# Sequence 1's ends behind the loop, and ScalarE and VectorE in written order, in the second MLP products of an encoder trunk

## The chip, the cores and the metric

The kernel runs on one core of a Trainium2 chip. The metric is the device time of one execution in microseconds (us). TensorE is PE, VectorE is DVE, ScalarE is ACT, GpSimd is POOL and SyncE is SP.

## The reference, cut to what matters

Two sequences (q = 0 and 1) of 512 tokens and 1024 features pass through two layers. Layer 0 mixes by a Fourier transform, layer 1 by attention. Each is followed by an MLP with squared ReLU:

```python
def sq_relu_mlp(h, w_up, w_down):
    a = jnp.maximum(h @ w_up, 0)
    return (a * a) @ w_down

for i in range(DEPTH):
    x = x + (fourier_mix(...) if i == 0 else gqa_attention(rms_norm(x, ...), ...))
    x = x + sq_relu_mlp(rms_norm(x, mlp_norm[i]), w_up[i], w_down[i])
return rms_norm(x, final_norm)
```

The change lies in the product with `w_down` of both layers and in what follows it: the QKV projection of layer 1's attention behind layer 0, a last small projection and the final norm behind layer 1.

## The kernel before

Every matmul of the MLP is done three times on a 128x512 tile. A 32-bit operand is split into a rounded high half and the rest, the low half: ACT copies the high half, then DVE subtracts it (`split`, lines 85 to 87). The product is high x high, high x low and low x high (`product`, line 907), with the weights stationary, so the third matmul of a product is the first to read the weights' low half.

The two sequences are not multiplied apart. Weights and activations are seen as 2 x 2 blocks, and seven products of sums of blocks take the place of eight. For the second MLP product these are `b11` and `b21` (class `Row`: two products of 12 matmuls) and `t1`, `t3`, `t2`, `b22`, `t4` (class `Sums`: five products, 60 matmuls). `second_product` goes over four groups of the inner dimension and, in each, over four column blocks m = 0 to 3. One turn of its loop is an item: the sums of one m, and in most items a row product of an m of the next group. In the last group the item of m = 1 has the last row (84 matmuls), those of m = 2 and 3 have none (60 each).

Within an item the weights of the next one are made ready. Three transfers fetch its raw blocks into a pool of five tiles. Then `sum_23` (two subtractions on DVE, lines 1183 and 1184), `split_12`, `sum_4` (line 1190), `split_4` and `split_3` follow. `split_3` makes `s3`, which the second product of the next item reads, and `a22`, which the fifth reads. Results leave PSUM by DVE adds (line 1113). One of the five goes to `e[m]`, a part that three blocks of the residual share. `xs[q, m]` is the residual; when all is done for a column block, `finish(m)` adds `e[m]` to one half of `xs[0, m]` (line 1253) and to both halves of `xs[1, m]` (line 1254), and calls `ready(m)`.

In layer 0 `ready` makes, for both sequences, the two halves of the operand `hT` of the QKV projection (`make_h`: a scaled copy on ACT, line 90, and DVE's half, line 91) and the squares for its norm (ACT, line 160, added up on POOL, line 164), and parks the residual in HBM on SP's queue (line 193). In the same last steps `late` fetches the four tiles of the weights of v (line 1359) and splits them.

Behind the loop `begun` does six of the eight steps of the inner dimension for v and k of sequence 0 (72 matmuls), then `token_scale` sums the squares (line 172), and a loop over the tiles finishes the projection, sequence 0 first.

Most of the order is found by a list scheduler, which simulates the engines and takes, engine by engine, the earliest instruction in program order that is ready. Inside `tc.manual_schedule(engines=...)` the instructions of the engines named keep the order in which they are written; others may still be placed between them. In the loop of `second_product` only PE is held so.

Of the kernel before, what the change touches and what calls it, by code (L numbers as in the profile page):

```python
# [12 lines left out]
F32 = mybir.dt.float32  # L13
# [6 lines left out]
P = 128  # L20
D = 1024
S = 512
NSEQ = 2
NT = S // P
KC = D // P
# [19 lines left out]
def trunk_kernel(ctx, tc, x_in, xt_in, y_out, tables, rope, gfour, gcol, grow, gfin,  # L45
                 w_four, w_nyq, w_qkv, w_o, w_a22, w_up, w_row2, w_row4, w_sum2, w_sum4, w_down):
    nc = tc.nc
# [17 lines left out]
    def slot(shape, dt):  # L65
        return act.tile(shape, dt, tag="u4", name=nm("u"))
# [18 lines left out]
    def split(dst_hi, dst_lo, src, eng=nc.vector):  # L85
        nc.scalar.copy(dst_hi, src)  # L86
        eng.tensor_sub(dst_lo, src, f32(dst_hi))  # L87
# [23 lines left out]
    def lent():  # L111
        return slot([P, 1024], F32R), slot([P, 1024], F32R)
# [32 lines left out]
    xs, acc, apart = {}, {}, {}  # L145
# [38 lines left out]
    def make_h(q, fo, g0):  # L184

        h = slot([P, 2, 512], F32R)
        split_scaled(h[:, 0], h[:, 1], xt(q, fo), gc[:, g0 + fo : g0 + fo + 1])
        return h
# [3 lines left out]
    def put_away(q, i):  # L192
        nc.sync.dma_start(park[q, i], xs[q, i])
# [507 lines left out]
    ET = mybir.EngineType  # L701
    with tc.manual_schedule(engines={ET.PE, ET.Activation, ET.DVE, ET.Pool, ET.SP}):
# [128 lines left out]
        blocks = Blocks(0)  # L831
# [259 lines left out]
                pass  # L1091
            pairs[-1].out(*done, nc.vector)

    def second_product(l, blocks, rows, late=lambda: None, ready=lambda m: None):
        e, new = [], [True] * 4
        there = set()

# [152 lines left out]
        def finish(m):  # L1250
            left[m] -= 1
            if left[m] == 0:
                nc.vector.tensor_add(xs[0, m][:, 1], xs[0, m][:, 1], e[m])
                nc.vector.tensor_add(xs[1, m], xs[1, m], e[m].unsqueeze(1).broadcast_to([P, 2, 512]))
                ready(m)

        first_product(l, blocks, rows, ahead)
# [36 lines left out]
        def hook():  # L1294
            for x in later:
                x[0] += 1
            if later and later[0][0] > 2:
# [2 lines left out]
                put(op, h)  # L1300
                held[op] = g

        for k, (rows, sums) in enumerate(items):
            nrows, nsums = items[k + 1] if k + 1 < len(items) else ([], None)
            end = sums.m if sums.g == len(GROUPS[l]) - 1 else -1
            if end in (0, 2):
                late()
            with tc.manual_schedule(engines={ET.PE}):
                for r in rows:
                    r.first()  # L1310
                    if r.m == 3:
                        change("b11", r.g)
                for r in nrows:
                    r.load()
                hook()
                for i, op in enumerate(("t1", "t3", "t2", "b22", "t4")):
                    sums.go(i)
                    if sums.m == 3:
                        change(op, sums.g)
                    if i == 0 and nsums:  # L1320
                        nsums.load()
                    if i == 1:
                        for r in rows:
                            r.second()
                            if r.m == 3:
                                change("b21", r.g)
                        if end == 1:
                            late()
                            late()
                        hook()  # L1330
                        for r in nrows:
                            r.split()
                    if i == 4 and nsums:
                        nsums.split_3()
                    hook()
                    if k == 0 and i in (2, 4):
                        change(ROW[i // 4], 0)
                    if i == 2 and nsums:
                        nsums.sum_23()
                        nsums.split_12()  # L1340
                    if i == 3 and nsums:
                        nsums.sum_4()
                        nsums.split_4()
            for r in rows:
                finish(r.m)
            finish(sums.m)


    hT, rs, wkv = [[], []], [], []
# [5 lines left out]
        rs.append(r)  # L1355

    def late():
        raw = slot([P, 1024], F32)
        nc.sync.dma_start(raw, w_qkv[2, len(wkv)])
        wkv.append(lent())  # L1360
        split(*wkv[-1], raw)

    def ready(m):
        for q in range(NSEQ):
            for fo in range(2 * m, 2 * m + 2):
                hT[q].append(make_h(q, fo, KC))
                square(q, fo)
            put_away(q, m)

    second_product(0, blocks, rows, late, ready)  # L1370

    gb = tm((P, 4, HD))
    nc.sync.dma_start(gb, grow.to_broadcast([P, 4, HD]))
# [197 lines left out]
    transposes = {(0, 0, 0): 0, (0, 1, 0): 1}  # L1571

    begun = [qkv(2, 0, t, wkv, 0, KC - 2) for t in range(NT)]
    token_scale(0)
    keeping, turned = keep(), iter(())
    ws = {2: wkv}
# [18 lines left out]
    def tile_qkv(cg, q, t):  # L1595
        if (cg, q, t) in transposes:
            transpose_k(transposes[cg, q, t])
        if (cg, q) == (2, 0):
            o = qkv(cg, q, t, ws[cg], KC - 2, KC, begun[t])
        else:  # L1600
            o = qkv(cg, q, t, ws[cg])
        if (cg, q, t) == (2, 0, 0):
            token_scale(1)
        r = rs[q][:, t : t + 1]
        if cg == 2:
            split_scaled(vt[q][0][:, t], vt[q][1][:, t], o[:, 256:], r)
            return norm_rope(o, NKV, rt["k"], [t], [kr[q][:, t]], scale=r)
        outs = [qr[q, 2 * cg + i][:, t] for i in range(2)]
        if (cg, q, t) != (1, 1, 1):
            return norm_rope(o, 4, rt["q"], [t], outs, scale=r)  # L1610
        raw = slot([P, 512], F32)
        nc.scalar.activation(raw, o, AF.Copy, scale=r)
        return norm_rope(raw, 4, rt["q"], [t], outs)
# [84 lines left out]
    with tc.manual_schedule(engines={ET.PE}):  # L1698
# [56 lines left out]
                blocks.first_lo(j - 3)  # L1755
        for i in range(2, 4):
            blocks.first_lo(i)
    second_product(1, blocks, rows)
    ats = []
    for f in range(2 * PLAIN):  # L1760
        raw = load_raw(plain[f], (P, 2, 512))
# [60 lines left out]
    with tc.manual_schedule(engines={ET.PE, ET.Activation, ET.DVE, ET.Pool, ET.SP}):  # L1822
        oa, ob, oc, oe = OutT(0, 4), OutT(1, 2), Out(2), Out(3)
        for fo in range(KC):
            project(0, fo, ws, [a[0] for a in ats])
            square(0, fo)
            oa.gain(fo)
        xtok = [tokens(2), tokens(3)]
        for fo in range(KC):
            project(1, fo, ws, [a[1] for a in ats], 256)  # L1830
            square(1, fo, 256, fo == KC - 1)
            ob.gain(fo)
            if fo == 1:
                oa.root()
            if fo == 3:
                oa.spread()
            if fo > 3:
                oa.write(fo - 4)

        x, z = xtok  # L1840
        y = slot([P, D], F32), slot([P, D], F32)
        groups = ((0, 512), (512, 768), (768, 1024))

        def tile(t, c0, c1, at=0, mid=lambda: None):
            o = ps()[:, : c1 - c0]
            for k in range(len(ats)):
                ak, wk = ats[k][1], ws[k]
                cols = slice(t * P, (t + 1) * P)
                mm3(o, ak[0][:, cols], ak[1][:, cols], wk[0][:, c0:c1], wk[1][:, c0:c1], k == 0, k == len(ats) - 1)
                if k == at:  # L1850
                    mid()
            return o

        def add(x, o, c0, c1):
            nc.vector.tensor_add(x[:, c0:c1], o, x[:, c0:c1])

        def write(x, y, r, i):
            sl = slice(i * 512, i * 512 + 512)
            nc.vector.scalar_tensor_tensor(y[:, sl], x[:, sl], r, gf[:, sl], ALU.mult, ALU.mult)

        o = [tile(2, 0, 512, 2, ob.root)]
        add(x, o[0], 0, 512)
        o.append(tile(2, 512, 1024, 0, ob.spread))
        oc.square(x[:, :512], 0)
        ob.write(0)
        add(x, o[1], 512, 1024)
        oc.square(x[:, 512:], 1)
        o = [tile(3, 0, 512)]
        ob.write(1)
        ob.write(2)  # L1870
        root = oc.root(1)
        for step in root[:2]:
            step()
        ob.write(3)
        for step in root[2:]:
            step()
        add(z, o[0], *groups[0])
        oe.square(z[:, :512], 0)
        write(x, y[0], oc.r, 0)
        o += [tile(3, *g) for g in groups[1:]]  # L1880
        add(z, o[1], *groups[1])
        oe.square(z[:, 512:768], 1)
        write(x, y[0], oc.r, 1)
        nc.sync.dma_start(y_out[2][:P], y[0])
        root = oe.root(2)
        add(z, o[2], *groups[2])
        oe.square(z[:, 768:], 2)
        nc.vector.tensor_mul(y[1][:, 512:768], z[:, 512:768], gf[:, 512:768])
        root[0]()
        root[1]()  # L1890
        nc.vector.tensor_mul(y[1][:, 768:], z[:, 768:], gf[:, 768:])
        for step in root[2:]:
            step()
        nc.scalar.activation(y[1][:, 512:], y[1][:, 512:], AF.Copy, scale=oe.r)
        nc.scalar.dma_start(y_out[2][P:, 512:], y[1][:, 512:])
        write(z, y[1], oe.r, 0)
        nc.sync.dma_start(y_out[2][P:, :512], y[1][:, :512])
# [151 lines left out]
```

## Time and profile before

| | |
|---|---|
| three runs | 1680.71, 1683.82, 1684.49 us; median 1683.82 |
| profiled execution | 1682.5 us, span 1680.5 us |
| granted TensorE clock, mean | 0.998 |
| PE busy | 1666.0 us, 99% of the span |
| DVE, ACT, POOL busy | 1258.9, 873.4, 394.5 us |

A timeline row gives start, duration, engine, line of the kernel, operation, output<-inputs, shapes and count; in brackets stands the idle time of the engine before it and what ended it. A row of the windows gives, for a stretch, its length, the busy time of PE, PE's weight load (PEld), DVE, ACT and POOL (with instructions), the granted clock of TensorE, the share of the DMA engines and GB/s. A row of the waits gives total, number of times and longest.

### The profile page before, as it was taken

Reading aid. Unit: us, or ns where it says so; the run is one execution under the profiler, and the core shown is the slowest. Engines: PE = TensorE matmul, PEld = TensorE weight load, DVE = VectorE, ACT = ScalarE, POOL = GpSimd, SP = SyncE. Lnnn points to the kernel's source line nnn. Section 1 sums busy time; section 2 is a strip of 40 time slices with the busy share of each in tenths; the row PEclk is TensorE's granted clock in tenths of the full one; section 3 lists DMA queues with packets and bytes.
Section 4 is the critical chain, followed back from the end, with each engine's and each line's share of the span. In section 5 each row is a group of like instructions: output and inputs, shape, how many; then the busy total and the mean of one; then the engine's idle time right before and its main releaser. Section 6 shows DMA issues by size and latency. Waiting matters only on the chain.

```text
span 1680.5 us, 22279 instructions
## 1 busy us (share of the span) xinstructions
PE 1666.0 (99%) x7845; PEld 1387.7 (83%) x7845; DVE 1258.9 (75%) x1848; ACT 873.4 (52%) x1537; POOL 394.5 (23%) x364
## 2 busy tenths in 40 slices
PE   9999999999999999999999999999999999999998
PEld 8988888888888888788878888888888888888887
DVE  8879776557786779869888877777855487878865
ACT  6766444456343425447698854554544553433334
POOL 3321443221000001325544303004422220000002
PEclk9999999999999999999999999999999999999999
DMA  9843655459775757425501146334544696757532
GB/s 310 262 151 111 209 194 182 145 176 371 242 231 170 254 171 225 168 65 196 168 1 39 63 164 224 124 114 160 209 156 155 226 367 203 232 158 237 176 102 100
DMA packets 122047, 302.99 MB, mean 180 GB/s; under 512 B 12200, under 2 KB 13352, under 8 KB 121936
## 3 DMA queue, kind: packets, MB, share of 16 engines
q1 hardware_dynamic: 98576, 254.05, 43.6%
q0 software_dynamic: 8960, 21.05, 5.9%
q10 hardware_dynamic: 14400, 26.48, 4.2%
q8 instruction: 61, 1.00, 0.2%
q14 instruction: 50, 0.41, 0.1%
HBM read 218.11 MB, written 82.38 MB: 179 GB/s over the span
## 4 chain that ended last, share of the span: by engine, by line
PE 87%; DVE 6%; ACT 3%; issue 2%; DMA 2%; POOL 0%; SPq 0%; DVEq 0%; ACTq 0%; POOLq 0%
PE ps L907 69%; PE ps L83 5%; PE ps L81 5%; PE ps L82 5%; PE ps L1482 1%; DVE w L87 1%; ACT t L1474 1%; ACT u L86 1%; DVE u L87 1%; DVE u L219 1%; DVE u L235 1%; DVE u L1113 0%; DMA u<-w_four 0%; DMA u<-x 0%; PE ps L172 0%
## 5 line engine op out<-in xcount | busy, mean ns | idle before, releaser
L907 PE MATMUL ps<-u,w 128*128 128x512 f32 x4944 | 1133.3, 390 | 2.9 <-DVE w L87 2.1
L907 PEld LDWEIGHTS ps<-u,w 128*128 128x128 f32 x4944 | 927.5, 188 | 199.1 <-DVE w L87 3.2
L86 ACT CAST w<-raw 128x1024 fp32r<-128x1024 f32 (+1 forms) x216 | 214.0, 996 | 310.9 <-PE ps L907 229.0
L87 DVE TENSOR_TENSOR w<-raw,w 128x1024 fp32r<-128x1024 f32 (+1 forms) x216 | 252.3, 1172 | 77.6 <-ACT w L86 77.3
L86 ACT CAST u<-u 128x1024 fp32r<-128x1024 f32 x144 | 145.2, 1049 | 83.8 <-PE ps L907 36.5
L87 DVE TENSOR_TENSOR u<-u,u 128x1024 fp32r<-128x1024 f32 x144 | 173.3, 1230 | 19.0 <-ACT u L86 17.9
L907 PE MATMUL ps<-u,u 128*128 128x512 f32 x600 | 143.1, 389 | 0.1
L1142 POOL DMA_DIRECT2D raw<-w_sum x32 | 27.7, 866 | 469.3 <-DMA raw<-w_sum 197.9
L1113 DVE TENSOR_TENSOR u<-ps,u 128x512 f32<-128x512 f32 x160 | 109.6, 686 | 37.2 <-PE ps L907 34.4
L1023 POOL TENSOR_TENSOR u<-u 128x512 f32<-128x512 f32 x28 | 37.7, 1345 | 424.7 <-ACT u L920 424.7
L907 PEld LDWEIGHTS ps<-u,u 128*128 128x128 f32 x600 | 112.5, 188 | 23.8 <-ACT u L938 0.5
L81 PE MATMUL ps<-u,u 128*128 128x512 f32 (+2 forms) x340 | 128.8, 381 | 0.4 <-ACT t L1474 0.3
L82 PE MATMUL ps<-u,u 128*128 128x512 f32 (+2 forms) x340 | 124.2, 366 | 0.4 <-DVE u L87 0.3
L83 PE MATMUL ps<-u,u 128*128 128x512 f32 (+2 forms) x340 | 124.4, 366 | 0.1
L164 POOL TENSOR_TENSOR t<-t,t 128x512 f32<-128x512 f32 (+1 forms) x54 | 77.8, 1446 | 190.6 <-ACT t L160 189.9
L919 ACT ACTIVATE t<-t 128x512 f32<-128x512 f32 x64 | 40.5, 632 | 109.8 <-DVE t L992 99.8
L87 DVE TENSOR_TENSOR u<-ps,u 128x512 fp32r<-128x512 f32 (+3 forms) x112 | 68.5, 635 | 7.9 <-ACT u L86 7.3
L83 PEld LDWEIGHTS ps<-u,u 128*128 128x128 f32 x340 | 64.2, 189 | 10.5 <-DVE u L448 0.5
L81 PEld LDWEIGHTS ps<-u,u 128*128 128x128 f32 x340 | 64.3, 189 | 10.1 <-ACT u L86 1.5
L82 PEld LDWEIGHTS ps<-u,u 128*128 128x128 f32 x340 | 64.4, 189 | 9.2 <-DVE u L87 1.4
L979 DVE TENSOR_TENSOR t<-ps,u 128x512 f32<-128x512 f32 x32 | 22.0, 688 | 60.5 <-PE ps L907 52.7
L1476 POOL TENSOR_SCALAR t<-t,s 128x512 f32<-128x512 f32 x64 | 47.3, 740 | 74.0 <-DVE s L1475 60.1
(260 smaller groups left out, 2029.7 us busy)
## 6 DMA issues: line engine op xcount, KB each, us to landing
raw<-w_up SPq DMA_DIRECT2D x80, 512.0 KB, 4.6
u<-spill_t SPq DMA_DIRECT2D x60, 512.0 KB, 6.8
raw<-w_sum SPq DMA_DIRECT2D x56, 512.0 KB, 5.7
u<-spill_b SPq DMA_DIRECT2D x45, 512.0 KB, 6.2
spill_t<-u SPq DMA_DIRECT2D x84, 256.0 KB, 2.0
spill_b<-t ACTq DMA_DIRECT2D x60, 256.0 KB, 4.3
raw<-w_row SPq DMA_DIRECT2D x28, 512.0 KB, 5.2
park<-u SPq DMA_DIRECT2D x24, 512.0 KB, 4.5
```

Of the source, the lines that this page charges most:

```text
L81: nc.tensor.matmul(out, lh, rh, start=first, stop=False)
L82: nc.tensor.matmul(out, lh, rl, start=False, stop=False)
L83: nc.tensor.matmul(out, ll, rh, start=False, stop=last)
L86: nc.scalar.copy(dst_hi, src)
L87: eng.tensor_sub(dst_lo, src, f32(dst_hi))
L164: nc.gpsimd.tensor_add(acc[q][:, :n], acc[q][:, :n], s[:, :n])
L907: nc.tensor.matmul(o, w[x][:, sl], h[k][y], start=first and k + i == 0, stop=k == n - 1 and i == 2, skip_group_check=not first)
L919: nc.scalar.activation(t, src, AF.Relu)
L1023: eng.tensor_sub(t[:, 0], b12, b11)
L1113: nc.vector.tensor_add(x, o, x)
L1142: nc.gpsimd.dma_start(s[:, 1], w[:, 3], accum_op=ALU.add)
L1476: nc.gpsimd.tensor_scalar(p, p, sm_[:, :1], 1.0, ALU.mult, ALU.mult)
```

## The change

- The add of `e[m]` to `xs[1, m]` leaves `finish` and becomes a function `other(m)`, which `second_product` returns. In layer 0 `other` and `ready(m, 1)` are called for all four m behind `begun`; in layer 1 `other` is called in the first four steps of the last projection.
- `ready(m)` now does one sequence, and its square comes ahead of its `make_h`.
- In the items of m = 1, 2 and 3 of the last group ACT and DVE are held in written order like PE. The `finish` of an item's column blocks is written after the first product of the next item, and that of the last item behind the loop.
- `late` becomes a generator. Its five steps stand in the items of m = 1 (one), m = 2 (one) and m = 3 (three); each asks for one tile of v's weights and splits the tile asked for a step before.
- `token_scale(1)` moves behind the first tile of sequence 1.

```diff
-    def second_product(l, blocks, rows, late=lambda: None, ready=lambda m: None):
+    def second_product(l, blocks, rows, late=iter(()), ready=lambda m: None):
...
                 nc.vector.tensor_add(xs[0, m][:, 1], xs[0, m][:, 1], e[m])
-                nc.vector.tensor_add(xs[1, m], xs[1, m], e[m].unsqueeze(1).broadcast_to([P, 2, 512]))
                 ready(m)
...
+        done = []
         for k, (rows, sums) in enumerate(items):
             nrows, nsums = items[k + 1] if k + 1 < len(items) else ([], None)
             end = sums.m if sums.g == len(GROUPS[l]) - 1 else -1
-            if end in (0, 2):
-                late()
-            with tc.manual_schedule(engines={ET.PE}):
+            with tc.manual_schedule(engines={ET.PE, ET.Activation, ET.DVE} if end > 0 else {ET.PE}):
...
                     if i == 0 and nsums:
                         nsums.load()
+                    if i == 0 and end > 0:
+                        for m in done:
+                            finish(m)
+                        done = []
+                    if (end, i) in ((2, 0), (3, 0), (3, 1), (3, 2)):
+                        next(late, None)
                     if i == 1:
...
                         if end == 1:
-                            late()
-                            late()
+                            next(late, None)
                         hook()
...
-            for r in rows:
-                finish(r.m)
-            finish(sums.m)
+            done += [r.m for r in rows] + [sums.m]
+            if end < 0:
+                for m in done:
+                    finish(m)
+                done = []
+        with tc.manual_schedule(engines={ET.Activation, ET.DVE}):
+            for m in done:
+                finish(m)
+
+        def other(m):
+            nc.vector.tensor_add(xs[1, m], xs[1, m], e[m].unsqueeze(1).broadcast_to([P, 2, 512]))
+
+        return other
...
     def late():
-        raw = slot([P, 1024], F32)
-        nc.sync.dma_start(raw, w_qkv[2, len(wkv)])
-        wkv.append(lent())
-        split(*wkv[-1], raw)
-
-    def ready(m):
-        for q in range(NSEQ):
-            for fo in range(2 * m, 2 * m + 2):
-                hT[q].append(make_h(q, fo, KC))
-                square(q, fo)
-            put_away(q, m)
-
-    second_product(0, blocks, rows, late, ready)
+        raw = []
+        for u in range(5):
+            if u < 4:
+                raw.append(slot([P, 1024], F32))
+                nc.sync.dma_start(raw[u], w_qkv[2, u])
+            if u:
+                wkv.append(lent())
+                split(*wkv[-1], raw[u - 1])
+            yield
+
+    def ready(m, q=0):
+        for fo in range(2 * m, 2 * m + 2):
+            square(q, fo)
+            hT[q].append(make_h(q, fo, KC))
+        put_away(q, m)
+
+    other = second_product(0, blocks, rows, late(), ready)
...
     begun = [qkv(2, 0, t, wkv, 0, KC - 2) for t in range(NT)]
+    with tc.manual_schedule(engines={ET.Activation, ET.DVE}):
+        for m in range(4):
+            other(m)
+        for m in range(4):
+            ready(m, 1)
     token_scale(0)
...
-        if (cg, q, t) == (2, 0, 0):
+        if (cg, q, t) == (2, 1, 0):
             token_scale(1)
...
-    second_product(1, blocks, rows)
+    other = second_product(1, blocks, rows)
...
             oa.gain(fo)
+            if fo < 4:
+                other(fo)
```

## The prediction

> **What bounds the kernel now.** I read the page first, then the waits of TensorE (PE), then the windows, then PE and VectorE (DVE) in order of time around the only large wait.
>
> ```profile
> span 1680.5 us, 22279 instructions
> PE 1666.0 (99%) x7845; PEld 1387.7 (83%) x7845; DVE 1258.9 (75%) x1848; ACT 873.4 (52%) x1537; POOL 394.5 (23%) x364
> PE ps L907 <- DVE w L87: 2.1, 2, 1.9
> ```
>
> PE is busy for 99% of the span, so an edit pays only where it shortens a wait of PE, and costs only where it makes one. The largest wait is 1.9 us on a weight split of DVE (line 87). In time it lies here:
>
> ```profile
> 693.71 0.84 PE L907 MATMUL ps<-u,w 128*128 128x512 f32 x3
> 696.46 12.34 PE L907 MATMUL ps<-u,w 128*128 128x512 f32 x46 [1.91 <-DVE w L87]
> 708.64 0.39 PE L81 MATMUL ps<-u,u 128*128 128x512 f32 x1
> 724.96 0.95 PE L172 MATMUL ps<-ones,t 128*128 128x2 f32 x8
> 694.04 1.22 DVE L1254 TENSOR_TENSOR u<-u,t 128x1024 f32<-128x1024 f32 x1
> 695.19 1.22 DVE L87 TENSOR_TENSOR w<-raw,w 128x1024 fp32r<-128x1024 f32 x1
> ```
>
> From 708.64 to 724.96 run the 72 matmuls of `begun`: 0.2267 us each, the pace of an undisturbed PE. The three matmuls from 693.71 end their turn at 694.39; the next starts at 696.46, which is 2.07 late, when the split at 695.19 ends. On DVE an add for sequence 1 (line 1254) went ahead of it. The 46 matmuls from there to 708.64 take 12.18 us, where 46 x 0.2267 is 10.43: another 1.75 is lost. The windows show to what:
>
> ```profile
> 697.00:698.00 1.00, 1.00 (x5) 0.81 (x4) 0.96 (x3) 0.18 (x1) 0.00 (x0) 0.84 1.18 320
> 700.00:701.00 1.00, 1.00 (x4) 0.80 (x3) 0.69 (x1) 0.02 (x1) 1.00 (x1) 0.50 0.79 168
> 702.00:703.00 1.00, 1.00 (x6) 0.81 (x6) 0.00 (x0) 0.00 (x0) 1.00 (x2) 1.00 0.70 287
> ```
>
> The granted clock (the figure ahead of the DMA share) is 0.50 up to 701, and 1.00 again by 702. So this place costs 2.07 + 1.75 = 3.82 us, and no edit here can win much more. 46 matmuls before the loop's end is the third matmul of the second product of the last item (m = 3): the first that needs the low half which `split_3` makes. That item would have begun 14 x 0.2267 earlier, at 691.2, the one before it (60 matmuls) at 677.6, and the one with the last row (84) at 658.6. This is layer 0; layer 1 has no such wait.
>
> **What the change takes away.** In layer 0, from these items, four adds of 1.22 (line 1254) and, for sequence 1, eight split halves on DVE, eight squares and eight scaled copies on ScalarE (ACT) and seven adds on GpSimd (POOL). The add at 694.04 is one of them. The wait of 2.07 and its 1.75 of low clock go if nothing takes their place: -3.82.
>
> **What the written order adds.** In the last three items DVE must now do: the add of the third product, `sum_23`, `split_12`, the add of the fourth, `sum_4`, `split_4`, the add of the fifth, `split_3`, where the scheduler before was free to do the sums for the next item as soon as their weights had come. Durations, from the item before (m = 0) in the same loop, DVE, then ACT:
>
> ```profile
> 652.85 0.69 DVE L1184 TENSOR_TENSOR raw<-raw 128x512 f32<-128x512 f32 x1
> 653.45 0.69 DVE L1113 TENSOR_TENSOR t<-ps,t 128x512 f32<-128x512 f32 x1
> 654.05 0.68 DVE L1190 TENSOR_TENSOR raw<-raw,raw 128x512 f32<-128x512 f32 x1
> 654.70 1.23 DVE L87 TENSOR_TENSOR w<-raw,w 128x1024 fp32r<-128x1024 f32 x1
> 656.71 0.69 DVE L87 TENSOR_TENSOR w<-raw,w 128x512 fp32r<-128x512 f32 x1
> 657.32 1.22 DVE L1254 TENSOR_TENSOR u<-u,t 128x1024 f32<-128x1024 f32 x1
> 653.61 1.06 ACT L86 CAST w<-raw 128x1024 fp32r<-128x1024 f32 x1 [1.94 <-DVE raw L1184]
> 656.06 0.62 ACT L86 CAST w<-raw 128x512 fp32r<-128x512 f32 x1 [1.39 <-PE ps L907]
> 1621.53 0.69 DVE L1113 TENSOR_TENSOR u<-ps,u 128x512 f32<-128x512 f32 x1 [0.41 <-PE ps L907]
> 1624.05 0.39 PE L81 MATMUL ps<-u,w 128*128 128x512 f32 x1
> ```
>
> An add or a 512-wide step lets the next begin after 0.60 (653.45 to 654.05), a 1024-wide split after about 1.14; an instruction that reads the result of the one before waits for its end (0.69); ACT starts 0.07 after the sum it needs (653.54 to 653.61), DVE 0.03 after ACT (654.67 to 654.70). An add starts 0.20 after its product: the product before the last ended 12 x 0.2267 ahead of 1624.05, at 1621.33, and its add began at 1621.53. Counted from the end of the third product: add starts 0.20; `sum_23` starts 0.80, its second half 1.49, ends 2.18; ACT's copy for `split_12` 2.25 to 3.31; DVE's half 3.34, next at 4.48; add of the fourth to 5.08; `sum_4` ends 5.76; ACT's copy 5.83 to 6.45; DVE's half 6.48, next at 7.09; add of the fifth (its product ended at 5.44) to 7.69; `split_3` ends 8.91. What a late low half costs is seen in layer 1's projection, where a split that ends late holds one matmul:
>
> ```profile
> 1625.34 1.22 DVE L87 TENSOR_TENSOR w<-raw,w 128x1024 fp32r<-128x1024 f32 x1
> 1626.62 0.19 PEld L83 LDWEIGHTS ps<-u,w 128*128 128x128 f32 x1 [0.34 <-DVE w L87]
> 1626.95 0.39 PE L81 MATMUL ps<-u,w 128*128 128x512 f32 x1
> ```
>
> It ends at 1626.56; the matmul due at 1624.05 + 11 x 0.2267 = 1626.54 slips and its follower starts at 1626.95, not 1626.77: 0.18 lost. So the loss is the split's end plus 0.16 less the due time. In the new order the third matmul of the next item's second product is due 24 + 14 matmuls after the third product: 8.61. Loss 8.91 + 0.16 - 8.61 = 0.46 us. This chain stands in items m = 1 and m = 2 of both layers, so four times. Two of its steps wait for ACT (1.16 and 0.72).
>
> Two of the four are worse. In layer 0, m = 2, `finish(1)` and the first weight of v stand ahead. From the item's start: add of the first product 2.92, `finish` add to 4.21, ACT square and scaled copy to 5.5, DVE's half to 6.2, split of the weight to 7.6, add of the second to 8.2: just under the 8.36 at which the third's add can start. But a POOL add beside it stretches DVE's work on SBUF operands:
>
> ```profile
> 685.09 7.77 POOL L164 TENSOR_TENSOR t<-t,t 128x512 f32<-128x512 f32 x4 [14.58 <-ACT t L160]
> 687.69 2.31 DVE L87 TENSOR_TENSOR w<-raw,w 128x1024 fp32r<-128x1024 f32 x1
> 689.93 1.78 DVE L91 SCALAR_TENSOR_TENSOR u<-u,gc,u 128x512 fp32r<-128x512 f32 x1
> 684.71 0.75 DVE L91 SCALAR_TENSOR_TENSOR u<-u,gc,u 128x512 fp32r<-128x512 f32 x1
> ```
>
> The half of 0.75 took 1.78 there and the split of 1.22 took 2.31. One POOL add still falls there: between 0 and 0.75; I take 0.3, since it overlaps only one step. In layer 1, m = 2, the scheduler may still place the splits of `ats`, which are not in written order, into the two waits for ACT:
>
> ```profile
> 1597.38 1.06 ACT L86 CAST u<-raw 128x1024 fp32r<-128x1024 f32 x1 [1.95 <-DMA raw<-plain]
> 1601.99 1.21 DVE L87 TENSOR_TENSOR u<-raw,u 128x1024 fp32r<-128x1024 f32 x1
> ```
>
> One that fits the wait of 1.16 costs nothing; one that meets an add costs its 1.14 and delays ACT's copy besides. Ends 0 and 1.3; I take 0.4, nearer the fitting one, as each comes with its own transfer and only one or two meet the chain. Together: 4 x 0.46 + 0.3 + 0.4 = 2.54.
>
> **What is moved and stays hidden.** Sequence 1 now follows the loop, beside the 16.3 us of `begun`, 0.8 of sums and 5.4 of the rest of q = 0: its h is first read 22.6 us after the loop. DVE needs until 3.9 for the last `finish`, 4.6 for the four adds, ACT from 5.2 on about 1.2 for each of eight squares and copies, to 14.8; DVE's last half to 17, or 23 if POOL stretched all eight to 1.78, while the last of them is read only 4 us after the first. Cost 0. DVE has the room:
>
> ```profile
> 720.00:730.00 10.00, 10.00 (x54) 8.55 (x53) 4.07 (x21) 1.22 (x5) 0.00 (x0) 1.00 0.18 52
> 1629.90 0.69 DVE L891 TENSOR_TENSOR u<-ps,u 128x512 f32<-128x512 f32 x1 [2.06 <-PE ps L83]
> ```
>
> In layer 1 the four adds go into the projection, where DVE idles 2.06 between two adds and each takes 1.22: 0. The parking of sequence 1 on SP's queue goes later with its data; behind it stand only loads of the QKV stage. The weights of v are asked for a step ahead:
>
> ```profile
> 696.85 0.64 SPq L1359 DMA_DIRECT2D u<-w_qkv  x1
> 703.59 1.05 ACT L86 CAST u<-u 128x1024 fp32r<-128x1024 f32 x1 [3.57 <-DMA u<-w_qkv]
> ```
>
> Before, the last came 6.7 after its issue, ACT idled 3.57 for it, and PE did not wait. Now ACT and DVE stand still behind such a split, but in the last item only adds follow it, and the banks these free are not needed by `begun`. Cost 0, and 0 gained.
>
> **Sum.** -3.82 + 2.54 = -1.28. The profiled execution took 1682.5 (span 1680.5 and 2.0 around it), so 1681.2 against it. It lies 1.3 below the median of 1683.82; the four executions shown average 1682.9, and against that the forecast is 1681.6.
>
> **A rule beside the rows.** The clock fell after a gap of 1.91 (above) and not after one of 0.73:
>
> ```profile
> 1047.32 0.96 PE L907 MATMUL ps<-u,w 128*128 128x512 f32 x3 [0.73 <-DVE u L1688]
> 1048.00:1049.00 1.00, 1.00 (x6) 0.82 (x5) 1.00 (x2) 0.63 (x2) 0.93 (x1) 1.00 0.00 0
> ```
>
> So none of the four new waits as priced should lower it, and one that grows towards 1.9 adds 1.75. [...]
>
> **Rivals.** (1) *Nothing is late.* The chain misses by 0.46 of 8.9; should steps overlap a little more than I read, all four waits vanish: -3.82, 1679.1. Chance 0.34. (2) *The chain overruns and the clock falls* (slower): the waits in m = 2 reach 1.2 in layer 0 and 1.76 in layer 1, past the point, somewhere between 0.73 and 1.91, at which the clock halves: 0.92 + (1.2 + 1.75) + (1.76 + 1.75) - 3.82 = +3.56, 1686.5. For it: both upper bounds above; against it: both must fall together. 0.15. (3) *Sequence 1's h is late*: PE waits ahead of its first v tile; it decides once the 17 to 23 us pass 22.6 by more than 4; a wait of 4 with a low clock behind it gives 1681.6 + 5.7 = 1687.3. 0.04. (4) *The loop's wait stays*, because the last weights and not DVE's load set it: 1682.9 within 1. 0.05. [...] 0.02. The forecast has 0.40.
>
> **Numbers.** 0.2% is 3.4 us, about what a measurement of this kernel can tell from no change. Rival 1 lies beyond it (0.34 faster), 2 and 3 on the other side (0.19 slower), the forecast, 4 and 5 between (0.47 same). The range runs from rival 1 less the 1.9 by which runs shown lie about their middle, 1677.2, to rival 2, 1686.5.
>
> **What would show it.** Right: no wait of 1.9 at the last item and granted clock 1.00 there; four short PE waits on DVE's `w` (line 87) of 0.3 to 0.9 at the second products of the last two items of both layers; line 1254's work beside `begun` and the projection. Wrong: no PE wait there (rival 1), windows with clock 0.50 behind them (rival 2), or a wait ahead of the first tile of q = 1.

## The result, and the profile after

The changed kernel takes 1693.7 us in the median (1692.3 to 1698.3), against 1682.8 for the kernel before in the same comparison: the ratio is 1.0072 [1.0060, 1.0083], slower by about 11 us. The forecast was 1681.6 with a range to 1686.5. The profiled execution took 1694.4 us.

The page of the changed kernel and the waits of PE in it (total, number, longest):

```profile
span 1692.6 us, 22297 instructions
PE 1669.7 (99%) x7845; PEld 1387.7 (82%) x7845; DVE 1260.0 (74%) x1848; ACT 872.4 (52%) x1537; POOL 391.7 (23%) x364
...
PE ps L1468 <- POOL u L1457: 3.8, 1, 3.8
PE ps L907 <- DVE w L87: 3.8, 6, 1.0
...
PE ps L907 <- DVE t L1113: 1.6, 1, 1.6
...
PE ps L907 <- ACT w L86: 0.7, 2, 0.4
```

DVE, ACT and POOL do as much as before; the span grew by 12.1 while PE's busy time grew by 3.7. In order of time PE of the changed kernel shows:

```profile
681.33 13.56 PE L907 MATMUL ps<-u,w 128*128 128x512 f32 x58 [0.64 <-DVE w L87]
695.27 0.73 PE L907 MATMUL ps<-u,w 128*128 128x512 f32 x2 [0.38 <-ACT w L86]
697.01 10.72 PE L907 MATMUL ps<-u,w 128*128 128x512 f32 x46 [1.01 <-DVE w L87]
707.57 0.39 PE L81 MATMUL ps<-u,u 128*128 128x512 f32 x1
...
757.34 1.33 PE L1468 MATMUL ps<-ident,u 128*128 128x128 f32 x5 [3.85 <-POOL u L1457]
...
1559.81 3.02 PE L907 MATMUL ps<-u,w 128*128 128x512 f32 x12 [1.63 <-DVE t L1113]
...
1608.58 11.46 PE L907 MATMUL ps<-u,w 128*128 128x512 f32 x48 [0.42 <-DVE w L87]
1620.56 2.57 PE L907 MATMUL ps<-u,w 128*128 128x512 f32 x10 [0.53 <-DVE w L87]
1623.49 0.73 PE L907 MATMUL ps<-u,w 128*128 128x512 f32 x2 [0.36 <-ACT w L86]
1625.23 10.73 PE L907 MATMUL ps<-u,w 128*128 128x512 f32 x46 [1.00 <-DVE w L87]
1635.79 0.39 PE L81 MATMUL ps<-u,w 128*128 128x512 f32 x1
```

The wait of 1.91 is gone, and the foretold waits are there: the second products of the last two items of both layers wait for DVE's `w` (0.64, 1.01, 0.42 and 1.00). Counted back from the end of each loop, three more stand beside them that were not foretold: in the last item of both layers the first matmul of the same second product waits for the high half, ACT's `w` (0.38 and 0.36), and in layer 1 the first product waits for its low half too (0.53). The largest wait, 3.85, lies where none was foretold: in the QKV stage, at the transposes of k, which wait for POOL's addition in the fourth k tile.

To say where time goes I cut each span at three places: PE's start on `begun`, the sums of layer 1's MLP norm (16 matmuls of line 172 in a row), and the first matmul of the last projection. The table gives each stretch's difference from the profile of before (708.64, then 319.15 to 1027.79, then 596.26 to 1624.05), in us, each from one profiled execution:

| kernel | up to `begun` | QKV and attention | layer 1's MLP | time, median | ratio to before |
|---|---|---|---|---|---|
| changed | -1.07 | +6.60 | +6.21 | 1693.7 | 1.0072 [1.0060, 1.0083] |
| changed, profiled again | -0.37 | +7.29 | +3.84 | 1693.4, one run | |
| before, profiled again | -2.52 | -0.06 | +0.02 | 1679.9, one run | |
| free order | -4.06 | +2.29 | -0.06 | 1681.0 | 1.0002 [0.9993, 1.0011] |
| order in layer 0 only | -1.08 | +7.34 | +5.08 | 1689.4 | 1.0053 [1.0034, 1.0073] |
| norm early | -0.74 | +3.43 | +3.83 | 1689.4 | 1.0050 [1.0035, 1.0065] |
| ends in the loop | +8.30 | +0.03 | +4.69 | 1696.2 | 1.0086 [1.0069, 1.0103] |
| free, norm early | -3.59 | +0.95 | +1.24 | 1680.9 | 0.9996 [0.9987, 1.0004] |
| split_3 first | -1.45 | +3.06 | +4.35 | 1688.7 | 1.0044 [1.0031, 1.0057] |
| free, norm early, tables behind | -4.45 | +0.54 | +0.94 | 1679.8 | 0.9990 [0.9981, 0.9999] |
| v ahead alone | -1.67 | +0.03 | +2.24 | 1681.0 | 0.9996 [0.9987, 1.0004] |
| no adds | -0.81 | +3.06 | +4.57 | 1690.2 | 1.0053 [1.0034, 1.0071] |
| sums early | -3.81 | +6.35 | +0.36 | 1686.7 | 1.0030 [1.0019, 1.0041] |
| sums early, tables behind | -3.98 | +6.93 | +5.26 | 1687.6 | 1.0034 [1.0021, 1.0046] |
| the same, norm early | -2.97 | +3.41 | -0.10 | 1683.0 | 1.0005 [0.9996, 1.0014] |

("Ends in the loop" is cut at the sums of line 172 of sequence 0 less the 16.32 that `begun` takes. Far ahead of anything that the change touches, at the first matmuls of line 180, the executions already lie between 115.7 and 117.0 us, so differences of up to 1.2 in the first column say nothing. The medians of the kernel before lie at 1680.8 to 1682.8 in the five comparisons.)

Layer 1's figure holds one wait that comes and goes: 1.63 at 1559.81 in the changed kernel, and 0 when the same kernel was profiled again. Without it the stretch still lost 3.84, in its last items. The +5.26 of "sums early, tables behind" is that wait too, 2.47 there with a low clock behind it (0.50 from 1559 to 1562).

### The profile page after: what moved, and what is told of

The parts are those of the page before. It is cut to its first block, busy times and chain, and to the rows that moved or that the text cites. A ratio compares the mean times of both kernels' runs of the same rounds, so it can differ in the third digit from the quotient of the medians.

```text
span 1692.6 us, 22297 instructions
## 1 busy us (share of the span) xinstructions
PE 1669.7 (99%) x7845; PEld 1387.7 (82%) x7845; DVE 1260.0 (74%) x1848; ACT 872.4 (52%) x1537; POOL 391.7 (23%) x364
## 4 chain that ended last, share of the span: by engine, by line
PE 85%; DVE 7%; ACT 3%; DMA 3%; issue 2%; POOL 0%; SPq 0%; ACTq 0%; DVEq 0%; POOLq 0%
PE ps L907 68%; PE ps L83 4%; PE ps L82 4%; PE ps L81 4%; PE ps L1499 1%; DVE w L87 1%; DMA raw<-w_sum 1%; ACT u L86 1%; ACT t L1491 1%; DVE u L87 1%; DVE u L1113 1%; DVE u L91 1%; ACT w L86 1%; DVE u L219 0%; DMA u<-x 0%
## 5 line engine op out<-in xcount | busy, mean ns | idle before, releaser
L160 ACT ACTIVATE t<-u 128x512 f32<-128x512 f32 (+1 forms) x64 | 38.4, 603 | 64.4 <-DVE u L1710 22.8
```

The lines of the kernel that those rows point to most:

```text
L160: nc.scalar.activation(s[:, :n], xt(q, fo)[:, :n], AF.Square)
```

## The experiments

**The order.** The written order taken away, from both layers and from layer 1 alone; the hold around the last `finish` goes with it.

```diff
-  with tc.manual_schedule(engines={ET.PE, ET.Activation, ET.DVE} if end > 0 else {ET.PE}):
+  with tc.manual_schedule(engines={ET.PE}):          # second run: "if end > 0 and l == 0"
```

> The change with ScalarE and VectorE free again in the last items of both layers; all else as in the change. Theory: the written order costs 2.75 us in layer 0's last items (waits of 0.64, 0.38 and 1.01) and 3.8 in layer 1's, and the place of sequence 1's ends costs 6.6 in the QKV stage whatever the order. Then this gains some 5 to 6.5 us on the change and is still 5 to 7 slower than before, with the wait of about 4 us at the transposes of k. Rival: the order in the last items is what makes the QKV stage late too (its queue of VectorE begins there). Then the wait at the transposes goes as well and this equals the kernel before within 2 us.

> The change with written order in layer 0 only. Theory: layer 1's last items lose 3.8 us only through the written order, so this is 3 to 4.5 us faster than the change and shows no wait of PE in layer 1's last two items; the 1.8 us wait in layer 1's third group (VectorE behind a sum whose raw weights come late) has nothing to do with the order and may be there or not. Rival: layer 1's waits come from the four adds of sequence 1 moved into the projection, or from its transfers; then they stay and this is the change within 1.5 us.

Free order gives back the whole loss: no wait in the last items of either layer, and 4.3 of the 6.6 in the QKV stage too, which my theory had put down to the moved work alone. With the order kept in layer 0 only, the waits of layer 1's last items go (its +5.08 is a wait of 2.58 in the third group with a low clock behind it, 0.50 from 1563 to 1565) and a wait of 4.25 stays at the transposes. So the QKV stage pays for the order in layer 0.

**The norm of sequence 1, and the ends.**

```diff
-        if (cg, q, t) == (2, 1, 0):
+        if (cg, q, t) == (2, 0, 0):
             token_scale(1)
```

> The change with the norm of sequence 1 (token_scale(1)) back behind the first v tile of sequence 0. Theory: the wait at the transposes of k has two parts, 4 to 5 us because sequence 1's eight halves stand on VectorE ahead of the first v tile's evacuation, and about 2 because the norm of sequence 1 now comes between k's third and fourth tile; this takes away the second: wait about 2 us, 1.5 to 3 us faster than the change. Rival 1: the moved norm is all of it: no wait, 6.6 us faster. Rival 2: the norm early stands on VectorE behind sequence 1's halves anyway: within 1 us of the change.

> The change with sequence 1's adds, squares and halves back in the loop (both layers) and its norm back at its old place; the written order and the new steps for v's weights stay. Theory: the QKV stage loses nothing (no wait at the transposes), but in layer 0 the halves of sequence 1 lengthen VectorE's chain in the last two items to waits of 1.5 to 2.5 us each with low clock behind one or two: layer 0's last items 2 to 5 us slower than in the change, the whole 2 to 4 us faster than the change. Rival: the order of VectorE in the QKV stage is spoilt by the held order in the loop: the wait at the transposes stays at 3 to 4 us and this is slower than the change.

The second run also has `other` and both `ready` in `finish` again. The early norm takes away 3.2 of the 6.6. With the ends back in the loop the QKV stage costs nothing (+0.03), so what it loses in the changed kernel comes from moving them. But in written order they cost 8.3 in the loop, with waits of 2.86 and 2.20: order and ends in the loop don't go together.

**Free order with repairs.** The norm early; then also the 16 steps that make the rope tables moved behind `ready(m, 1)`.

> The changed kernel with VectorE and ScalarE in free order in the last items of both layers, and with sequence 1's norm back at its old place, behind the first v/k tile instead of behind the fifth. Theory (the written order and the moved norm are two separate losses): layer 0 as in the free-order run, the pre-started work of line 1254's sums beginning at 704.6, no wait in the last items of either layer; of the 2.3 us that the attention projections still lost there (waits 0.66 and 1.04) about 2 go; time some 1678.5 to 1679.5 beside 1681 to 1682.8 of the kernel before. Rival (the attention projections lose because sequence 1's adds and halves stand behind the loop, wherever the norm stands): the 2.3 us stay or move to a wait for the norm's sums, and the time stays at that of the kernel before within 0.2%.

> The free-order kernel with the norm early, and the 16 rope-table steps (6.58 us on VectorE, behind 3.20 us idle for the grow transfer) written behind sequence 1's halves instead of ahead of them. Theory (VectorE stands idle for the transfer and then in the tables while the halves could run): the halves start about 5 to 9 us earlier against the sums, the first v evacuation comes at about 6 us behind the sums instead of 9.8, what is left of waits in the attention projections goes (0 to 0.5 us in all); time 0 to 1.5 us under the kernel with the norm early alone, 1677.5 to 1679. Rival (the tables are needed by the first rotated k tile and become late themselves): a PE wait at the transposes of 1 to 3 us takes their place.

The QKV loss shrinks to 0.95 and 0.54, less than hoped, and the last version is the only one whose interval lies on the faster side, by 0.1%, and it just leaves out 1.

**v's weights alone.** The kernel before with the new `late`.

> The kernel before with one part of the change alone: v's four weight tiles loaded one step ahead of their splits. Sequence 1's ends stay in the loop, the order stays free. Theory (the 2.07 us wait in layer 0's last item came from sequence 1's ends, so taking them out is what gained): that wait and the low clock behind it stay, at 1.5 to 4 us, and the time stays within 0.2% of the kernel before. Rival (the wait came from where the weights' loads and splits stood): the wait goes, the pre-started work begins 4 us earlier and the time is 1677 to 1679.

The 1.91 gives way to waits of 0.65 and 0.28, and the granted clock of the whole execution averages 0.999. That alone does not refute the theory, because the kernel before shows as little when it is profiled a second time (next).

**Both kernels profiled again.**

> The kernel before, unchanged, profiled a second time. Question: does the wait in layer 1's third group (a sum's last load late, then a first product's add late: 1.63 in the changed kernel's profile, 0 in the profile before) come and go with the run? Theory (it hangs on how fast the transfers land in that execution): a wait of 0 to 2.5 can show here too, and the wait of 1.91 in layer 0's last item with its low clock shows again. Rival (it comes from the change): none here, as in the first profile.

> The changed kernel, unchanged, profiled a second time. Theory (layer 1's third group depends on the execution, the other losses on the program): the waits of layer 0's last items (0.64, 0.38, 1.01), of the transposes (3.85) and of layer 1's last items (0.42, 0.53, 0.36, 1.00) come back within 0.3 each; the third group's wait is anything from 0 to 2.6. Rival (the third group's wait is the change's): 1.4 to 1.9 again.

PE in the kernel before, profiled again, and the window at that place:

```profile
695.54 8.70 PE L907 MATMUL ps<-u,w 128*128 128x512 f32 x37 [0.43 <-DVE w L87]
...
697.00:698.00 1.00, 1.00 (x6) 1.00 0.89 291
```

The wait on which my gain rested is 0.43 here, with no low clock (1.00). The changed kernel repeats its own: 0.64, 0.38, 1.00, then 4.12, then 0.41, 0.70, 0.37, 1.01, and none in the third group. That last wait is not the change's: "v ahead alone", which leaves layer 1's code as in the kernel before, shows 2.07 there, behind a transfer that held DVE's sum for 3.57.

**What makes the written order late.** Three edits that keep it. First, `split_3` ahead of `sum_4` and `split_4`; then the four adds of line 1357 left out, so that sequence 1's residual lacks them; then the sums written where the free order runs them. This third edit is given as the order of the steps, not as the code's lines (i is the product behind which a step stands, from 0):

```diff
# in the last items of both layers
-  i == 2: sum_23, split_12      i == 3: sum_4, split_4      i == 4: split_3
+  i == 1: sum_23, sum_4         i == 2: split_12   i == 3: split_3   i == 4: split_4
```

> The changed kernel, written order kept, but in the last items of both layers the split of the third operand is written ahead of sum_4 and split_4, behind the third product's add and split_12. Theory (the chain before split_3 is too long, whatever the scheduler slots into it): the waits of the second product on VectorE's w (0.64 and 1.01 in layer 0, 0.42, 0.53 and 1.00 in layer 1) fall to under 0.2 each, layer 0's loss of 2.75 us falls to about 1 and layer 1's 3.76 to about 1.5; the attention projections keep their 6.6; time some 1689 to 1690. Rival (what is slotted in ahead, sequence 1's adds and the splits of the attention output, sets the lateness): the waits only move to the first product's w or to the fourth's, 0.5 to 1 each, and the time stays above 1692.

> The changed kernel without sequence 1's four adds of layer 0 (1.22 us each on VectorE, line 1357; sequence 1's residual then lacks that part of layer 0). They are the only work that the scheduler slotted into the written order of layer 0's last items. Theory A (these adds lengthen the chain): the waits 0.64, 0.38 and 1.01 fall to zero or to one of under 0.3, and the pre-started work begins at 705 or before instead of 707.6. Theory B (the written chain itself is too long, the prediction's 0.46 a time): two waits of 0.3 to 0.5 remain and the work begins at 706 to 706.5. By either the attention projections lose about as much as before, 4 to 6.6, and layer 1 as much, so the time is 1690 to 1693.

> The changed kernel, written order kept, but in the last items of both layers the sums are written one and two products earlier, where the free order runs them: sum_23 and sum_4 behind the second product's add, split_12 behind the third's, split_3 behind the fourth's, split_4 behind the fifth's. Theory (written order is no loss by itself; it loses because these steps stand later in it than their inputs and their users allow, VectorE idle for 2.03 us twice an item ahead of them): no wait over 0.2 in layer 0's last items, 0.5 at most in layer 1's, the transposes' wait as in the run with split_3 ahead (2.7) or shorter; time 1683 to 1687. Rival (what is inserted, the adds and the splits of the attention output, makes any written order late): waits of 0.4 to 1 remain at the second products, the time 1688 or more.

Without the adds the waits are 0.41, 0.36 and 0.77: each low half comes 0.23 sooner and no more, so the chain itself is too long. `begun` starts at 707.83, later than either theory had it, because that execution was already 0.79 behind the changed kernel's at line 180 (116.82 against 116.03); from there the way is 0.53 shorter, and the waits are 0.49 shorter. (The QKV stage lost 3.06 there, less than expected.) With `split_3` first, waits of 0.53 and 0.34 are left in layer 0, and layer 1 gets a new one of 1.53 on ACT, with 0.72 on DVE behind it. With the sums early there is no wait over 0.2 in the last items of either layer, though the adds and the splits of the attention output still go between. What is left is a wait of 4.57 at the transposes. DVE's work for the last item of layer 0 in the changed kernel, then the same sums in free order:

```profile
687.90 0.67 DVE L1113 TENSOR_TENSOR t<-ps,t 128x512 f32<-128x512 f32 x1
688.50 0.67 DVE L1183 TENSOR_TENSOR raw<-raw,raw 128x512 f32<-128x512 f32 x1
689.21 0.69 DVE L1184 TENSOR_TENSOR raw<-raw 128x512 f32<-128x512 f32 x1
691.06 1.23 DVE L87 TENSOR_TENSOR w<-raw,w 128x1024 fp32r<-128x1024 f32 x1 [1.16 <-ACT w L86]
692.20 0.68 DVE L1113 TENSOR_TENSOR u<-ps,u 128x512 f32<-128x512 f32 x1
692.80 0.68 DVE L1190 TENSOR_TENSOR raw<-raw,raw 128x512 f32<-128x512 f32 x1
693.40 1.22 DVE L1357 TENSOR_TENSOR u<-u,t 128x1024 f32<-128x1024 f32 x1
694.53 0.68 DVE L87 TENSOR_TENSOR w<-raw,w 128x512 fp32r<-128x512 f32 x1
695.14 0.68 DVE L1113 TENSOR_TENSOR u<-ps,u 128x512 f32<-128x512 f32 x1
695.74 1.22 DVE L87 TENSOR_TENSOR w<-raw,w 128x1024 fp32r<-128x1024 f32 x1
```

```profile
674.86 0.69 DVE L1113 TENSOR_TENSOR u<-ps,u 128x512 f32<-128x512 f32 x1 [1.33 <-PE ps L907]
675.57 0.69 DVE L1183 TENSOR_TENSOR raw<-raw,raw 128x512 f32<-128x512 f32 x1
...
677.32 0.69 DVE L1184 TENSOR_TENSOR raw<-raw 128x512 f32<-128x512 f32 x1
...
678.52 0.68 DVE L1190 TENSOR_TENSOR raw<-raw,raw 128x512 f32<-128x512 f32 x1
```

The sums are the same ones: done by 679.20 in free order, 693.48 in the written one. Written behind the third product's add, eight steps must follow it one after another, with two waits for ACT, one of which the add of line 1357 fills here.

**What is left of the QKV loss.** The sums early, with the tables behind; then with the norm early too.

> The written order with its sums early (no wait left in the last items of either layer, 1686.7), and the 16 rope-table steps written behind sequence 1's halves; the norm of sequence 1 stays behind the fifth v/k tile. Theory (what is left, a wait of 4.57 at the transposes with a clock of 0.67 behind it, comes from the halves standing behind the tables, the tables behind the grow load, and that behind the last stores on SP's queue): the halves start some 5 us earlier, that wait falls under 1.5 and the clock stays at 1.00; the attention projections lose 1 to 2.5 instead of 6.35; time 1681 to 1683. Rival (the moved norm sets it, because it goes between two k tiles): the wait stays over 2.5, time 1685 or more.

> As the run before it, and sequence 1's norm back behind the first v/k tile. All three losses found are then mended and the written order kept in both layers. Theory: no PE wait over 0.7 from the last row to the transposes, the attention projections lose 0.3 to 1 against the kernel before; time 1679 to 1681, no slower than the free-order kernel with the same two repairs (1679.8) by more than 1.5. Rival (with the halves late, the early norm holds PE ahead of its sums, 0.9 as in the run with the norm early alone, or the tables come late for the first k tile): 1682 to 1685.

The tables were not it, the norm was. POOL's third and fourth k additions and PE's wait, with the norm late, then POOL's same two and PE's sums, with the norm early:

```profile
746.01 1.65 POOL L1457 TENSOR_TENSOR u<-t,t 128x256 f32<-128x256 f32 x1 [3.20 <-DVE t L1455]
752.73 1.64 POOL L1457 TENSOR_TENSOR u<-t,t 128x256 f32<-128x256 f32 x1 [5.06 <-DVE t L1455]
754.41 1.33 PE L1468 MATMUL ps<-ident,u 128*128 128x128 f32 x5 [3.83 <-POOL u L1457]
```

```profile
746.70 1.65 POOL L1457 TENSOR_TENSOR u<-t,t 128x256 f32<-128x256 f32 x1 [3.20 <-DVE t L1455]
751.55 2.25 POOL L1457 TENSOR_TENSOR u<-t,t 128x256 f32<-128x256 f32 x1 [3.20 <-DVE t L1455]
725.95 1.05 PE L172 MATMUL ps<-ones,t 128*128 128x2 f32 x8 [1.51 <-POOL t L164]
```

The late norm falls between the third and the fourth tile and makes their distance 6.72 instead of 4.85. Early, it makes PE wait 1.51 for sequence 1's squares instead, with a low clock of 0.50 behind; the rival was right there. In the free order with the same two repairs the last square is added up 4.9 us earlier (721.02 against 725.89) and neither wait is left: ACT's squares start behind the loop's last add (line 1253), which stands behind the splits of v's weights in the written order and ends at 711.24 there, at 706.29 in the free one. So the written order still costs some 2.5 us with everything else mended (ratios of 1.0005 and 0.9990).

## Why the prediction was wrong

By place, the sum had -2.60 up to `begun` (-3.82 + 1.22), 0 in the QKV stage and +1.32 in layer 1's MLP; the two profiles show -1.07, +6.60 and +6.21.

**The gain of 3.82 was one execution's.** The wait was 1.91 with 1.75 lost to a clock of 0.50 in the first profile and 0.43 at 1.00 in the second; two profiles do not tell how often it comes. Most loops without any wait reach `begun` at 704.2 to 705.1 (free order, sums early), some 4 us ahead of the first profile of before but only 1.0 to 1.9 ahead of the second.

**The chain was found and mis-sized.** Place and releaser of the four waits were right. From the third add's start to the end of `split_3` I counted 8.71; above it is 9.06 (687.90 to 696.96), 9.16 in the item before. Line 1357's add, which I had sent behind the loop, stands in it: the scheduler puts it into the wait for ACT, and leaving it out gave 0.23 a time. I also priced only the low half of the second product's weights; in the last items their high half is late as well (0.36 and 0.38 on ACT), and in layer 1 the first product's low half (0.53). Layer 0's 1.22 was 2.0 of waits, with PE some 3 us behind the free order at `begun`; layer 1's 1.32 was 2.31 of waits and about 4 of time. The splits of `ats`, my reason for a larger loss in layer 1, do stand in its chain: it takes 9.15 in the first profile (1616.02 to 1625.17) and 9.51 in the second, where ACT copies one of them just ahead of the weights. No run takes them out of the written order, so their share is not shown; with the sums early they are still there and no wait is.

**"Cost 0" for sequence 1's ends failed, and is the largest miss (+6.60).** I asked when PE reads sequence 1's h, and there PE indeed never waited. I left out who stands in line on DVE between: the rope tables, the halves, the norm and then every evacuation of sequence 0's v and k. The changed kernel, ACT, SP, DVE and POOL:

```profile
705.54 1.05 ACT L86 CAST u<-u 128x1024 fp32r<-128x1024 f32 x1 [4.59 <-DMA u<-w_qkv]
712.96 2.34 SPq L1390 DMA_DIRECT2D t<-grow  x1
718.37 6.58 DVE L1399 SCALAR_TENSOR_TENSOR u<-raw,t 128x128 f32<-128x128 f32 x16 [3.20 <-DMA t<-grow]
724.87 5.48 DVE L91 SCALAR_TENSOR_TENSOR u<-u,gc,u 128x512 fp32r<-128x512 f32 x5
749.97 0.15 DVE L135 TENSOR_SCALAR s<-ps 128x4 f32<-128x4 f32 x1
755.64 1.64 POOL L1457 TENSOR_TENSOR u<-t,t 128x256 f32<-128x256 f32 x1 [5.00 <-DVE t L1455]
```

**"Cost 0" for v's weights overlooked the same queue.** Their last two loads land at 705.5 and 706.8 (698.8 and 700.1 in free order). The held splits stand ahead of the loop's last adds on DVE, the stores of the residual follow those adds on SP, and the grow load stands behind the stores: it is asked for at 712.96, against 706.65 in free order. I had said of SP's queue that only loads of the QKV stage stand behind; this one had work behind it. The kernel before asked for it no sooner, at 713.32, with no wait behind it: sequence 1's halves stood ahead of the tables there (done at 717.90, the tables from 718.05). Moving the tables behind the halves gained nothing by itself (+6.93 against +6.35). So this is a link that the rows show, and no run shows what v's loads or the late grow load cost alone. Then come tables, halves, and the norm at 749.97 between two k tiles. That the moved ends, the written order and the late norm act together is shown by taking each away: +0.03 with the ends back in the loop (and the norm early), +2.29 in free order, +3.43 with the norm early alone.

**The clock: right for the waits in the loops, wrong as a rule.** In the changed kernel no wait up to 1.01 in the loops lowered it, as foretold (1.00 in the windows from 682 to 683, 696 to 698 and 1624 to 1627). But the size of a gap alone does not tell. Windows of PE alone behind the gap of 1.51 (sums early, tables behind, norm early), then of all engines behind one of 2.73 (split_3 first) and inside and behind the 3.85 (changed):

```profile
728.00:729.00 1.00, 1.00 (x5) 0.69 0.00 0
729.00:730.00 1.00, 1.00 (x3) 0.50 0.00 0
731.00:732.00 1.00, 1.00 (x5) 0.61 0.82 279
```

```profile
756.00:757.00 1.00, 1.00 (x8) 0.91 (x8) 0.97 (x3) 0.00 (x0) 0.00 (x0) 1.00 0.80 238
```

```profile
755.00:756.00 1.00, 0.00 (x0) 0.00 (x0) 1.00 (x4) 0.09 (x1) 0.36 (x1) 0.83 0.00 0
758.00:759.00 1.00, 1.00 (x6) 0.90 (x5) 0.95 (x2) 0.01 (x1) 0.00 (x0) 0.50 0.76 287
762.00:763.00 1.00, 1.00 (x5) 0.82 (x4) 1.00 (x3) 0.32 (x1) 0.65 (x1) 0.76 0.20 76
```

My estimate of a low stretch, from the 0.50 of these rows and the 1.75 lost in 3.40 of the kernel before, is half of the part of it in which PE works, and with that the QKV losses come out as wait plus clock within 0.4: 1.51 + 1.70 against +3.41, 2.73 + 0 against +3.06; for the 3.85 the low stretch runs from 755.66 to 762.48, of which PE could use the part from 757.34, 2.6: 6.4 against +6.60.

Of the rivals, the second (the chain overruns and the clock falls) had the sign and a chance of 0.15, but neither the place nor the cause: the waits in the loops stayed at a granted clock of 1.00. The third foresaw that sequence 1's ends come late, with the wrong reader: PE's wait came at the transposes of sequence 0, behind DVE's line, not at sequence 1's first tile.

## What to carry to other kernels

Moving work "behind the loop" is priced by the queue of the engine that gets it, down to the last instruction that used to stand there with slack, and not by the first reader of its result. Writing down an order cost nothing inside the loops once each step stood as early as its inputs allow (here the sums, two products earlier); written in the order in which one reads the algorithm, it takes away the early starts that a scheduler had found. What it holds back at the loop's end is paid for in the stage behind: with the sums early the QKV stage still lost 6.35, in free order 2.29. And a gain that rests on one wait in one profile should be looked up in a second execution of the same kernel before it is counted.

## What the runs showed of the hardware

The low stretches of the granted clock, at 0.50, last 3.40 (728.38 to 731.78 from the windows above, and 697.7 to 701.1 in the kernel before) or 6.82 (755.66 to 762.48 in the changed kernel), which is twice as long. Gaps of 1.51 and 1.91 brought one, and so did the 2.86 and 2.20 of "ends in the loop" (falls at 693.48 and 713.96). Gaps of 2.07 ("v ahead alone", 1.00 from 1551 to 1562) and 2.73 ("split_3 first", 1.00 from 753 to 761) did not, nor did the 1.63 of the changed kernel (layer 1's third group, 1.00 from 1559 to 1563). What decides which gap lowers the clock is not shown.

The clock falls once more at the end of these three programs, when PE has nothing left. PE of the changed kernel, of "v ahead alone" and of "split_3 first":

```profile
1687.00:1688.00 1.00, 0.00 (x0) 0.74 0.42 168
```

```profile
1677.00:1678.00 1.00, 0.00 (x0) 0.93 0.00 0
```

```profile
1682.00:1683.00 1.00, 0.00 (x0) 0.87 0.00 0
```

So it falls at 1687.48, 1677.86 and 1682.74; in the changed kernel that is 2.4 behind the end of PE's last matmul (1685.06).

Also open is the third group's wait in layer 1, 0 to 2.58 for kernels with the same code there, behind the last of three transfers for a sum. It differs between executions of one program, and I did not find what sets it.
